# Splitting the next group's first weight item earlier, with six separate hi/lo homes and raw weights released singly

## Chip, cores and metric

The kernel runs on one core of one Trainium2 chip. The metric is device time in microseconds (us) of one execution. The time before is the median of three runs.

## What is computed

Two decoder layers on 512 tokens of width 1024, all in float32. Each layer has a half-step SwiGLU feed-forward part, a mixer (a gated linear recurrence and a sliding-window attention, each with a gate) and a second half-step feed-forward part, all with RMS norms around them:

```
def swiglu(h, w_gate, w_up, w_down):
    return (jax.nn.silu(h @ w_gate) * (h @ w_up)) @ w_down
...
  x += 1/2 * post(SwiGLU_1(pre(x)))
  h  = pre(x);  P = h @ W_in
  x += post( (sigmoid(gA)*A + sigmoid(gB)*B) @ W_out )
  x += 1/2 * post(SwiGLU_2(pre(x)))
```

D_MODEL is 1024 and D_FF is 2816, so that the gate and the up weight have 22 column blocks of 128 each. The weights of one feed-forward part are 66 units of 512 KB, each read from HBM once.

## The kernel before

**Products in three parts.** Every float32 operand is split into a rounded part hi and a rest lo (both float32r), and a product is three matmuls: hi·hi, hi·lo and lo·hi (`mm3`, helper line L116 in the profile). A weight unit is a tile of 128 x 1024 float32. SyncE loads it (L247) into one of four raw buffers (`W32` = 4, tag `w32`). Splitting it takes a copy on ScalarE that writes hi (L354), and for lo one of two ways. Either VectorE subtracts hi from the raw unit (L363), or, for the kinds "v", "a" and "d", ScalarE writes the negative of the raw unit into lo (L358) and GpSimd issues a DMA that adds the raw unit to it (L361, an accumulating DMA from SBUF to SBUF). There are six hi and six lo buffers (`WS` = 6), so at most six split items are in flight.

**The pair phases.** Most of a feed-forward part's gate and up blocks go through `fast` (L1073) and `sevenths` (L1036): two raw units u and u+1 and two halves of the tokens make one 2 x 2 block product that is done with seven half-size products in place of eight. A *group* is one such pair. Its four items are

- a: unit u as it is, lo by the accumulating DMA of 512 KB; products p1 and p2
- b: sums on VectorE (L340, L341), lo by VectorE (L363); products p5 and p7
- c: two more sums (L347, L348), lo by VectorE; products p6 and p4
- d: half of unit u+1, lo by an accumulating DMA of 256 KB; product p3

TensorE takes them in the order a b c d, 84 matmuls of 128 x 256 per group, in an order written out by hand. After c, VectorE combines the results in PSUM (L1063, L1065, L1069, L1070), and ScalarE takes a SiLU (L1084). The next group's items are called a', b', c', d' below. There are four pair phases, one per feed-forward part: the first with 15 groups, the others with 19. In the profile they lie at about 88.7–233.4, 728.0–915.2, 1062.3–1247.0 and 1741.6–1928.0 us. The mixer has four further groups per layer in its gates part (`gates`, L189).

**Order of the work.** `split` (L324) takes the items in the order in which TensorE uses them; `ahead` (L373) calls it whenever fewer than four items (`AHEAD` + 1) lie ahead of the one in use and fewer than six are in flight. In the pair phases (`tight`), ScalarE's and VectorE's instructions of a split are kept in program order, so where `split` is called decides what stands ahead of what on ScalarE, VectorE and GpSimd. Each of these engines and each DMA queue works through its list in order. A raw unit is given back, and the load that takes its buffer issued, at the end of d for both units of the group (L366–371).

Of the kernel before, what the change touches and what calls it, by code (L numbers as in the profile page):

```python
# [8 lines left out]
F32R = mybir.dt.float32r  # L9
# [6 lines left out]
P = 128  # L16
D = 1024
# [19 lines left out]
W32, WS, AHEAD, TAIL, FIRST, EARLY, LATE = 4, 6, 3, 4, 7, 4, 8  # L37
# [9 lines left out]
def trunk(ctx: ExitStack, tc: tile.TileContext, xin, wall, gains, lbT, hgain, sinks, c_dist, c_mask, c_ident, out):  # L47
    nc = tc.nc
    cp = ctx.enter_context(tc.tile_pool(name="cp", bufs=1))
    sb = ctx.enter_context(tc.tile_pool(name="sb", bufs=1))  # L50
# [9 lines left out]
    def nm(s):  # L60
        seq[0] += 1
        return f"{s}_{seq[0]}"
# [18 lines left out]
    class Order:  # L81
        def __init__(self):
            self.t = 0.0
            self.rest = 0.0
            self.cos = []
# [73 lines left out]
    class Stream:  # L159
        def __init__(self):  # L160
            self.n, self.wall = 0, 0
            self.items = []
            self.raw, self.dma = {}, 0
            self.done, self.flight = 0, 0
            self.cur, self.c = 0, 0
            self.src = {}
            self.pinned = False
            self.most = AHEAD
            self.tight, self.gate = False, None
            self.side, self.freed = [], 0  # L170
            self.part = {}

        def plain(self, n, kind="u", at=0):
# [84 lines left out]
        def quarter(self, it):  # L258

            q, u, v, h = it.q, it.u, it.u + it.n, (slice(0, S), slice(S, D))  # L260

            def sums(o, x, y, op):
                for c in range(2):
                    pin(nc.vector.tensor_tensor(o[c], x[c], y[c], op=op))  # L264

            def raw(i):
                self.load(i + 1)
                return [self.raw[i][:, c] for c in h]

            def leave(i):  # L270
                self.raw.pop(i)
                self.freed += 1
                self.load(self.freed + W32)

            if it.kind in ("p1", "p2"):
                w = raw((u if it.kind == "p1" else v) + q)
            elif it.kind in ("p3", "p5"):
                w = self.b22[q]
            elif it.kind == "p7":

                w = self.b12[q]
                if q == 0:
                    sums(w, w, self.b22[q], ALU.add)
            else:
                w = self.b12[q]
            it.hi, it.lo = (sb.tile([P, D + 64], F32R, tag=t, name=nm(t), bufs=WS)[:, it.at : it.at + D] for t in ("whi", "wlo"))
            for c in range(2):
                i = nc.scalar.copy(it.hi[:, h[c]], w[c])  # L288
                if self.pinned:
                    pin(i)  # L290
            if it.kind == "p7" and q + 1 < it.n:
                sums(self.b12[q + 1], self.b12[q + 1], self.b22[q + 1], ALU.add)
            elif it.kind == "p6":
                sums(self.b22[q], self.b22[q], w, ALU.add)
            for c in range(2):
                pin(nc.vector.tensor_tensor(it.lo[:, h[c]], w[c], it.hi[:, h[c]].bitcast(F32), op=ALU.subtract))  # L296
            if it.kind == "p7":

                sums(w, raw(u + q), w, ALU.subtract)
                leave(u + q)  # L300
            elif it.kind == "p5":
                self.b22[q] = None
                if q + 1 < it.n:
                    sums(self.b12[q], raw(v + q), self.b12[q], ALU.add)
                    leave(v + q)
            elif it.kind == "p4":
                self.b12[q] = None
                if q == 0:
                    i = it.n - 1
                    sums(self.b12[i], raw(v + i), self.b12[i], ALU.add)  # L310
                    leave(v + i)
            self.done += 1
            self.flight += 1
# [5 lines left out]
        def product(self):  # L319
            if self.gate:  # L320
                self.gate()
                self.gate = None

        def split(self):  # L324
            it = self.items[self.done]
            if it.kind[0] == "p":
                return self.quarter(it)
            u, last = it.u, it.kind in "uvd"
            self.load(u + (1 if it.kind in "uv" else 2))
            it.hi, it.lo = (sb.tile([P, D + 64], F32R, tag=t, name=nm(t), bufs=WS)[:, it.at : it.at + D] for t in ("whi", "wlo"))  # L330
            w, h = self.raw[u], (slice(0, D // 2), slice(D // 2, D))
            cols = (slice(0, D),)
            if it.kind == "u" and u < 2:
                cols = h
            if it.kind in "bcd":
                v = self.raw[u + 1]
            if it.kind == "b":

                self.t13 = sb.tile([P, D], F32, tag="tt", name=nm("tt"), bufs=2)
                pin(nc.vector.tensor_tensor(self.t13[:, h[0]], w[:, h[0]], v[:, h[0]], op=ALU.add))  # L340
                pin(nc.vector.tensor_tensor(self.t13[:, h[1]], v[:, h[0]], v[:, h[1]], op=ALU.add))  # L341
                w = self.t13
                self.product()
            elif it.kind == "c":

                t = sb.tile([P, D], F32, tag="tt", name=nm("tt"), bufs=2)
                pin(nc.vector.tensor_tensor(t[:, h[0]], self.t13[:, h[0]], v[:, h[1]], op=ALU.add))  # L347
                pin(nc.vector.tensor_tensor(t[:, h[1]], t[:, h[0]], w[:, h[1]], op=ALU.add))  # L348
                w = t
            elif it.kind == "d":  # L350
                w = v
                cols = h[1:]
            for c in cols:
                i = nc.scalar.copy(it.hi[:, c], w[:, c])  # L354
                if u < 6 or self.pinned or self.tight:
                    pin(i)
                if it.kind in "vad":
                    i = nc.scalar.mul(it.lo[:, c], w[:, c], -1.0)  # L358
                    if self.pinned or self.tight:
                        pin(i)  # L360
                    nc.gpsimd.dma_start(it.lo[:, c].bitcast(F32), w[:, c], accum_op=ALU.add)  # L361
                else:
                    self.hold(nc.vector.tensor_tensor(it.lo[:, c], w[:, c], it.hi[:, c].bitcast(F32), op=ALU.subtract))  # L363
            self.done += 1
            self.flight += 1
            if last:  # L366
                nu = u + (1 if it.kind in "uv" else 2)
                for i in range(u, nu):
                    self.raw.pop(i)
                    self.freed += 1  # L370
                self.load(self.freed + W32)

        def ahead(self):  # L373
# [2 lines left out]

        def need(self, i):
            self.ahead()
            while self.done <= i:
                assert self.flight < WS  # L380
                self.split()
            return self.items[i]
# [117 lines left out]
    def pair_split(v, how=split):  # L500
        return how(v, to=(big(F32R, [P, 2, S // 2]), big(F32R, [P, 2, S // 2])))
# [13 lines left out]
    class First(Quarters):  # L515
# [44 lines left out]
        def sums(self):  # L560

            k = len(self.x56)
            a = []
            for i in range(2):
                f = xs[k + 4 * i]
                nc.vector.scalar_tensor_tensor(f, f, g_sb[:, 0, 0, k + 4 * i : k + 4 * i + 1], self.rb, op0=ALU.mult, op1=ALU.mult)
                a.append([f[:, c] for c in HALF])
            self.x124.append([])
            for v in (a[0][0], a[1][0], a[1][1]):
                x = big(F32R, [P, 2, S // 2])  # L570
                split(v, to=(x[:, 0, :], x[:, 1, :]))
                self.x124[k].append(x)
            for x, v in zip((self.x56, self.x37), quarter_sums(a[0][0], a[1][0], a[0][1], a[1][1])):
                x.append(pair_split(v))
# [74 lines left out]
    class Late:  # L649
# [20 lines left out]
        def first(self, k):  # L670
            x = big(F32R, [P, 2, S // 2])
            self.x1.append(split(self.src[k][:, HALF[0]], to=(x[:, 0, :], x[:, 1, :]), hold=pin))
# [979 lines left out]
```

## Time and profile before

| what | value |
|---|---|
| median of three runs | 2052.85 us (2051.64 to 2053.39) |
| profiled execution | 2052.22 us |
| span of its profile | 2050.4 us |
| TensorE busy | 2035.9 us, 99% |
| VectorE, ScalarE, GpSimd busy | 79%, 61%, 13% |
| granted TensorE clock | 0.999 |
| DMA, mean over the span | 160 GB/s |

The span is measured from the first to the last recorded instruction; 1.8 us of the execution lie around it. A timeline row has the start, the duration, the engine, the line and the operation, with output and inputs (buffer numbers left out), and in brackets the idle time ahead of it with what ended that. A window row has the stretch, its length, and for each engine the busy time and, in brackets with an x, the number of instructions. A row of DMA issues has the queue, the count, the size of each and the median time from issue to landing.

### The profile page before, as it was taken

How to read it: one execution, taken by the hardware profiler on the slowest of the kernel's cores; microseconds unless marked ns; L12 is line 12 of the kernel's file. 1: busy time of each engine (PE TensorE's matmuls, PEld its weight loads, DVE VectorE, ACT ScalarE, POOL GpSimd, SP SyncE). 2: the span in 40 equal slices, each digit the busy share in tenths (PEclk: the TensorE clock that was granted, in tenths of full speed). 3: DMA queues.
4: the chain of work that ended last, by engine and by line, in shares of the span. 5: the costliest groups of instructions: out<-in, count | busy, mean ns of one | idle time of the engine just before them, and what ended most of it. 6: DMA issues, size and time to landing. Idle time of an engine off the chain costs nothing. (4 is left out here: it accounts for less than half of the span.)

```text
span 2050.4 us, 36557 instructions
## 1 busy us (share of the span) xinstructions
PE 2035.9 (99%) x13553; PEld 1820.7 (89%) x13553; DVE 1623.6 (79%) x2894; ACT 1250.1 (61%) x2213; POOL 267.6 (13%) x318
## 2 busy tenths in 40 slices
PE   9999999999999999999999999999999999999998
PEld 8899978877888999998899998888778989999977
DVE  5887889767676778888988878987686858788888
ACT  7566687446355556658866566864554545665684
POOL 0111140000000011113201111400000100111140
PEclk9999999999999999999999999999999999999999
DMA  8577798322237367778757878872122563777794
GB/s 257 146 189 193 184 195 238 117 64 71 73 94 215 114 147 190 189 190 205 203 154 188 193 187 205 181 229 92 62 73 62 136 194 102 181 188 190 184 201 123
DMA packets 166802, 328.07 MB, mean 160 GB/s; under 512 B 19072, under 2 KB 85088, under 8 KB 166624
## 3 DMA queue, kind: packets, MB, share of 16 engines
q1 hardware_dynamic: 122416, 228.16, 33.2%
q0 software_dynamic: 44064, 97.54, 28.2%
q8 instruction: 106, 1.74, 0.3%
q14 instruction: 72, 0.59, 0.1%
q10 hardware_dynamic: 144, 0.05, 0.0%
HBM read 213.43 MB, written 14.73 MB: 111 GB/s over the span
## 5 line engine op out<-in xcount | busy, mean ns | idle before, releaser
L116 PE MATMUL acc<-s,whi 128*128 128x256 f32 (+1 forms) x4998 | 1027.5, 305 | 0.0
L116 PEld LDWEIGHTS acc<-s,whi 128*128 128x128 f32 x4998 | 794.7, 188 | 46.5 <-issue 3.2
L116 PE MATMUL acc<-s,wlo 128*128 128x256 f32 (+1 forms) x2488 | 757.0, 304 | 3.3 <-DMA wlo<-w 2.9
L116 PEld LDWEIGHTS acc<-s,wlo 128*128 128x128 f32 x2488 | 469.1, 189 | 28.7 <-DMA wlo<-w 5.0
L116 PE MATMUL acc<-whi,s 128*128 128x512 f32 x1360 | 442.4, 393 | 2.6 <-DVE s L433 1.8
L354 ACT CAST whi<-w 128x1024 fp32r<-128x1024 f32 (+1 forms) x310 | 286.5, 928 | 148.2 <-PE acc L116 105.2
L354 ACT CAST whi<-tt 128x1024 fp32r<-128x1024 f32 x160 | 168.0, 1050 | 250.2 <-DVE tt L348 164.7
L361 POOL DMA_DIRECT2D wlo<-w x178 | 154.0, 867 | 1235.6 <-DVE wlo L363 504.8
L116 PEld LDWEIGHTS acc<-whi,s 128*128 128x128 f32 x1360 | 255.0, 188 | 61.4 <-issue 3.2
L363 DVE TENSOR_TENSOR wlo<-tt,whi 128x1024 fp32r<-128x1024 f32 x160 | 196.0, 1225 | 131.9 <-ACT whi L354 126.0
L116 PE MATMUL acc<-wlo,s 128*128 128x512 f32 x680 | 266.4, 392 | 0.9 <-DVE wlo L296 0.9
L116 PE MATMUL aux<-s,whi 128*128 128x256 f32 (+1 forms) x1296 | 230.0, 280 | 0.0
L363 DVE TENSOR_TENSOR wlo<-w,whi 128x1024 fp32r<-128x1024 f32 (+1 forms) x132 | 157.3, 1205 | 73.9 <-ACT whi L354 73.6
L116 PEld LDWEIGHTS aux<-s,whi 128*128 128x128 f32 x1296 | 197.0, 188 | 1.1 <-issue 0.5
L116 PE MATMUL aux<-s,wlo 128*128 128x256 f32 (+1 forms) x648 | 181.1, 279 | 0.0
L116 PEld LDWEIGHTS acc<-wlo,s 128*128 128x128 f32 x680 | 127.8, 188 | 29.8 <-DVE wlo L296 5.1
L358 ACT ACTIVATE wlo<-w 128x1024 fp32r<-128x1024 f32 (+1 forms) x178 | 153.7, 863 | 0.0
L116 PE MATMUL aux<-whi,s 128*128 128x512 f32 x432 | 144.1, 391 | 0.0
L444 POOL DMA_DIRECT2D s<-s x128 | 111.1, 971 | 216.1 <-ACT s L432 98.1
L116 PEld LDWEIGHTS aux<-s,wlo 128*128 128x128 f32 x648 | 122.1, 188 | 0.5 <-DMA wlo<-w 0.2
L296 DVE TENSOR_TENSOR wlo<-s,whi 128x512 fp32r<-128x512 f32 x160 | 102.7, 685 | 9.9 <-ACT whi L288 6.3
L432 ACT CAST s<-s 128x512 fp32r<-128x512 f32 (+1 forms) x140 | 70.8, 547 | 44.8 <-DVE s L491 39.3
(184 smaller groups left out, 2468.7 us busy)
## 6 DMA issues: line engine op xcount, KB each, us to landing
w<-wall SPq DMA_DIRECT2D x267, 512.0 KB, 4.2
wlo<-w POOLq DMA_DIRECT2D x98, 512.0 KB, 5.2
w<-wall SPq DMA_DIRECT2D x224, 128.0 KB, 3.5
wlo<-w POOLq DMA_DIRECT2D x80, 256.0 KB, 3.3
s<-wall SPq DMA_DIRECT2D x128, 128.0 KB, 4.4
s<-s POOLq DMA_DIRECT2D x64, 256.0 KB, 4.9
x_d<-s SPq DMA_DIRECT2D x48, 256.0 KB, 4.1
s<-x_d SPq DMA_DIRECT2D x48, 256.0 KB, 5.1
```

The costliest lines, as they stand in the source:

```text
L116: nc.tensor.matmul(o, lhsT, rhs, start=start, stop=stop)
L296: pin(nc.vector.tensor_tensor(it.lo[:, h[c]], w[c], it.hi[:, h[c]].bitcast(F32), op=ALU.subtract))
L354: i = nc.scalar.copy(it.hi[:, c], w[:, c])
L358: i = nc.scalar.mul(it.lo[:, c], w[:, c], -1.0)
L361: nc.gpsimd.dma_start(it.lo[:, c].bitcast(F32), w[:, c], accum_op=ALU.add)
L363: self.hold(nc.vector.tensor_tensor(it.lo[:, c], w[:, c], it.hi[:, c].bitcast(F32), op=ALU.subtract))
L432: (hold or ws.hold)(nc.scalar.copy(hi, src))
L444: nc.gpsimd.dma_start(lo.bitcast(F32), src, accum_op=ALU.add)
```

## The change

It has three parts.

1. **Order of splits.** A plan replaces the running index: where an item a follows an item d, it is split ahead of the two items that come before it. The order a b c d a' b' c' d' becomes a b a' c d b' a'' c' d' and so on. TensorE's order is the same.
2. **Homes.** The six hi and lo buffers get tags of their own (`whi0` … `wlo5`). An item takes, of those whose last item is used up, the one whose item came first in TensorE's order; before, the pool gave the six out under one tag. `quarter` does the same.
3. **Raw units one by one.** Unit u is given back, and a load issued into its buffer, after c; unit u+1 after d.

```
+        def home(self, it):
+
+            k = min((k for k in range(WS) if not self.own[k] or self.own[k].left <= 0), key=lambda k: self.own[k].i if self.own[k] else -1)
+            self.own[k] = it
+            it.hi, it.lo = (sb.tile([P, D + 64], F32R, tag=f"{t}{k}", name=nm(t))[:, it.at : it.at + D] for t in ("whi", "wlo"))
+
         def split(self):
-            it = self.items[self.done]
+            if not self.plan:
+                for i, it in enumerate(self.items):
+                    it.i = i
+                    self.plan.append(i)
+                    if it.kind == "a" and self.items[i - 1].kind == "d":
+                        self.plan[i - 2 : i + 1] = [i, i - 2, i - 1]
+            it = self.items[self.plan[self.done]]
...
-            it.hi, it.lo = (sb.tile([P, D + 64], F32R, tag=t, name=nm(t), bufs=WS)[:, it.at : it.at + D] for t in ("whi", "wlo"))
-            w, h = self.raw[u], (slice(0, D // 2), slice(D // 2, D))
+            self.home(it)
+            w, h = self.raw.get(u), (slice(0, D // 2), slice(D // 2, D))
...
-            if last:
-                nu = u + (1 if it.kind in "uv" else 2)
-                for i in range(u, nu):
-                    self.raw.pop(i)
-                    self.freed += 1
+            if it.kind in "uvcd":
+                self.raw.pop(u + (it.kind == "d"))
+                self.freed += 1
                 self.load(self.freed + W32)
...
-            while self.done <= i:
+            while not hasattr(self.items[i], "hi"):
```

On ScalarE, one group of the first pair phase before: the copy of b', a copy out of PSUM (L1051), the copies of c' and d', the multiplication of d', then the pair of a'' (`whi_2036`, `wlo_2037`, from raw unit `w_336`), then the SiLU.

```order
L354 CAST whi_1936<-tt_1938 128x1024
L1051 COPY s_1931<-acc_1927 128x256
L354 CAST whi_1969<-tt_1971 128x1024
L354 CAST whi_2000<-w_317_1753 128x512
L358 ACTIVATE wlo_2001<-w_317_1753 128x512
L354 CAST whi_2036<-w_336_1878 128x1024
L358 ACTIVATE wlo_2037<-w_336_1878 128x1024
L1084 ACTIVATE m_2018<-m_2018 128x512
```

The same place of the changed kernel, where the split's copy is L367, its multiplication L371, the PSUM copy L1062 and the SiLU L1095:

```order
L367 CAST whi_1936<-tt_1938 128x1024
L1062 COPY s_1931<-acc_1927 128x256
L367 CAST whi_1969<-w_336_1878 128x1024
L371 ACTIVATE wlo_1970<-w_336_1878 128x1024
L367 CAST whi_1998<-tt_2000 128x1024
L367 CAST whi_2034<-w_320_1785 128x512
L371 ACTIVATE wlo_2035<-w_320_1785 128x512
L1095 ACTIVATE m_2016<-m_2016 128x512
```

The pair of instructions that reads `w_336`, the whole unit of a'', has moved from behind d' to ahead of c'. Nothing is added and nothing taken away.

On GpSimd, the accumulating DMAs of three groups in the same phase before; those of 128x512 belong to items d, those of 128x1024 to items a:

```order
L361 DMA wlo_1366<-w_217_1118 128x512
L361 DMA wlo_1402<-w_236_1243 128x1024
L361 DMA wlo_1493<-w_237_1245 128x512
L361 DMA wlo_1529<-w_256_1370 128x1024
L361 DMA wlo_1620<-w_257_1372 128x512
L361 DMA wlo_1656<-w_276_1497 128x1024
```

And of the changed kernel, where the line is L374:

```order
L374 DMA wlo_1335<-w_236_1243 128x1024
L374 DMA wlo_1400<-w_220_1150 128x512
L374 DMA wlo_1462<-w_256_1370 128x1024
L374 DMA wlo_1527<-w_240_1277 128x512
L374 DMA wlo_1589<-w_276_1497 128x1024
L374 DMA wlo_1654<-w_260_1404 128x512
```

Within each group the whole unit's DMA (`w_236`) now stands ahead of the half unit's (`w_220`, the same half unit as `w_217` of before under another number). VectorE's order in the pair phases and SyncE's order of loads are the same as before; in the mixer's gates part the rows of the two items move likewise on ScalarE, VectorE and GpSimd.

More of the change, by code (lines that the diff above doesn't have):

```diff
@@ L170, in __init__ @@
             self.side, self.freed = [], 0
+            self.own, self.plan = [None] * WS, []
             self.part = {}
@@ L322, in product @@
                 self.gate = None
+        def home(self, it):
+            k = min((k for k in range(WS) if not self.own[k] or self.own[k].left <= 0), key=lambda k: self.own[k].i if self.own[k] else -1)
+            self.own[k] = it
+            it.hi, it.lo = (sb.tile([P, D + 64], F32R, tag=f"{t}{k}", name=nm(t))[:, it.at : it.at + D] for t in ("whi", "wlo"))
         def split(self):
-            it = self.items[self.done]
+            if not self.plan:
[5 more added lines that the diff above has]
+            it = self.items[self.plan[self.done]]
             if it.kind[0] == "p":
                 return self.quarter(it)
-            u, last = it.u, it.kind in "uvd"
+            u = it.u
             self.load(u + (1 if it.kind in "uv" else 2))
-            it.hi, it.lo = (sb.tile([P, D + 64], F32R, tag=t, name=nm(t), bufs=WS)[:, it.at : it.at + D] for t in ("whi", "wlo"))
-            w, h = self.raw[u], (slice(0, D // 2), slice(D // 2, D))
+            self.home(it)
+            w, h = self.raw.get(u), (slice(0, D // 2), slice(D // 2, D))
             cols = (slice(0, D),)
```

## The prediction

> **What bounds the kernel now.** I read the page first, then the waits of TensorE, then windows over the four pair phases, and last one group in the timelines. The page's busy times and its two large DMA queues (packets, MB, share of 16 engines' span):
>
> ```profile
> PE 2035.9 (99%) x13553; PEld 1820.7 (89%) x13553; DVE 1623.6 (79%) x2894; ACT 1250.1 (61%) x2213; POOL 267.6 (13%) x318
> q1 hardware_dynamic: 122416, 228.16, 33.2%
> q0 software_dynamic: 44064, 97.54, 28.2%
> ```
>
> TensorE is busy nearly always, so there is little idle time to win. The queues give prices: q0, the accumulating DMAs, took 28.2% of 2050.4 us for 97.54 MB, 5.93 us per MB, so 3.1 us of all 16 engines for a 512 KB item and 1.55 us for 256 KB; q1, the loads, 680.7 us for 228.16 MB, 1.56 us per unit. What TensorE and its weight loads wait for of DMA (us, times, longest):
>
> ```profile
> PE acc L116 <- DMA wlo<-w: 2.9, 4, 1.6
> PEld acc L116 <- DMA wlo<-w: 5.0, 9, 1.8
> ```
>
> Not above 8 us, and the two lists overlap. But waiting is not all that a stage can lose. The four pair phases, then one stretch of 37 us, then five other stretches inside the phases:
>
> ```profile
> 88.70:233.40 144.70, 144.70 (x1262) 144.70 (x1261) 115.98 (x163) 88.99 (x122) 24.95 (x29) 1.00 0.79 191
> 728.00:915.20 187.20, 187.04 (x1599) 186.49 (x1599) 150.53 (x210) 115.22 (x158) 31.85 (x37) 1.00 0.78 188
> 1062.30:1247.00 184.70, 182.66 (x1599) 181.52 (x1598) 147.71 (x208) 113.16 (x156) 31.84 (x37) 1.00 0.77 187
> 1741.60:1928.00 186.40, 185.83 (x1599) 185.33 (x1598) 149.72 (x210) 115.03 (x158) 31.84 (x37) 1.00 0.78 189
> 147.00:184.00 37.00, 37.00 (x329) 37.00 (x328) 30.78 (x44) 22.22 (x30) 6.88 (x8) 1.00 0.79 186
> 184.00:234.00 50.00, 50.00 (x424) 49.91 (x423) 39.88 (x57) 32.02 (x45) 7.74 (x9) 1.00 0.78 194
> 747.00:758.00 11.00, 10.84 (x91) 10.44 (x89) 8.61 (x13) 6.36 (x9) 1.72 (x2) 1.00 0.77 211
> 786.00:915.00 129.00, 129.00 (x1096) 128.88 (x1095) 104.14 (x145) 79.81 (x109) 21.53 (x25) 1.00 0.78 190
> 1761.00:1801.00 40.00, 39.95 (x338) 39.74 (x337) 31.73 (x45) 24.61 (x33) 6.88 (x8) 1.00 0.79 192
> 1858.00:1928.00 70.00, 69.49 (x590) 69.29 (x589) 56.19 (x79) 44.16 (x61) 11.18 (x13) 1.00 0.78 193
> ```
>
> The same matmuls run at two rates under a granted clock of 1.00 throughout: 37.00/329 = 112.5 ns each at first, 129.00/1096 = 117.7 ns in the longest of the others. The slow rate sets in at one of the waits for an accumulating DMA and stays until the next; what decides it, the profile does not say. The five slow stretches are 300 us, and at about 3.8% cost some 11 us.
>
> How long should a phase be? One group as TensorE runs it: the first use of d's lo, the first of the next a's lo, and the same a in the group before.
>
> ```profile
> 117.50 0.28 PE L116 MATMUL acc<-s,wlo 128*128 128x256 f32 x1
> 125.66 0.28 PE L116 MATMUL aux<-s,wlo 128*128 128x256 f32 x1
> 127.02 0.28 PE L116 MATMUL acc<-s,wlo 128*128 128x256 f32 x1
> ```
>
> From a to a it is 127.02 − 117.50 = 9.52 us (84 matmuls; at the slow rate 84 x 117.7 ns = 9.89). By 9.52 us, 15 groups need 142.8 us and 19 need 180.9; the windows are 1.9, 6.3, 3.8 and 5.5 us longer, **17.5 us in all**. No change in these phases can win more. VectorE's own round shows where it begins:
>
> ```profile
> 98.75 0.68 DVE L1063 TENSOR_TENSOR m<-acc,s 128x512 f32<-128x512 f32 x1
> 108.51 0.68 DVE L1063 TENSOR_TENSOR m<-acc,s 128x512 f32<-128x512 f32 x1
> 118.22 0.68 DVE L1063 TENSOR_TENSOR m<-acc,s 128x512 f32<-128x512 f32 x1
> ```
>
> It takes 9.71 to 9.76 us per group, 0.19 more than a fast TensorE. Each group therefore eats 0.19 us of every margin, until the tightest is gone and TensorE waits.
>
> **The change part by part.** Which margin is tightest? ScalarE in one group (c, d, then the next a), GpSimd's two DMA issues (d, then a), and their issue-to-landing times (d, a, and the load issued at c):
>
> ```profile
> 113.22 0.36 ACT L1051 COPY s<-acc 128x256 f32<-128x256 f32 x1
> 115.99 1.05 ACT L354 CAST whi<-tt 128x1024 fp32r<-128x1024 f32 x1 [2.41 <-PE aux L116]
> 118.00 1.03 ACT L354 CAST whi<-w 128x1024 fp32r<-128x1024 f32 x1
> 118.94 1.06 ACT L358 ACTIVATE wlo<-w 128x1024 fp32r<-128x1024 f32 x1
> 118.39 0.86 POOL L361 DMA_DIRECT2D wlo<-w  x1 [6.96 <-DVE wlo L363]
> 120.29 0.86 POOL L361 DMA_DIRECT2D wlo<-w  x1 [1.03 <-DVE m L1069]
> wlo<-w POOLq DMA_DIRECT2D x1, 256.0 KB, 3.2
> wlo<-w POOLq DMA_DIRECT2D x1, 512.0 KB, 5.1
> w<-wall SPq DMA_DIRECT2D x1, 512.0 KB, 3.5
> ```
>
> Item a lands at 120.29 + 5.1 = 125.4 for a use at 127.02: margin 1.6. Item d lands at 118.39 + 3.2 = 121.6 for 125.66: margin 4.1. So a's DMA is the tight one, and d's has 2.5 us more.
>
> *Moving a ahead of c.* ScalarE idles 2.41 us before c's copy. The pair now starts where L1051 ends, at about 113.5; two instructions that start 0.94 apart end at about 115.5, 0.4 us before c's copy can start at 115.99. So c is not delayed, VectorE's round stays at 9.71, and a's DMA is issued 0.3 us after its multiplication, as at 120.29, at about 115.8: **4.5 us earlier**. It doesn't land 4.5 earlier, since it now shares the engines with the load issued at c. The trace has one such meeting, in the third phase, where a DMA of an a at 1116.11 fell upon a load, both landed late, and TensorE waited:
>
> ```profile
> wlo<-w POOLq DMA_DIRECT2D x1, 512.0 KB, 6.2
> w<-wall SPq DMA_DIRECT2D x1, 512.0 KB, 5.7
> 1122.32 0.38 PE L116 MATMUL acc<-s,wlo 128*128 128x256 f32 x1 [1.58 <-DMA wlo<-w]
> ```
>
> At 6.2 us a lands at 122.0, 3.4 us before it did: its margin becomes about 5.0.
>
> *What is late next: d.* Its issue stays at 118.39, but its DMA is now behind a's in GpSimd's queue. From below its landing does not move (3.2 us); from above it waits for a's whole landing at 122.0 and then takes its own 3.2, so 125.2, 3.6 later. I take 122.0 plus its 1.55 us of data plus a little for the completion, 123.8, **2.2 later**: margin 4.1 − 2.2 = 1.9. So the tightest margin is 1.9 in place of 1.6; from both sides between 0.5 and 4.1. This is nearly an exchange of one late wait for another.
>
> The Trainium skill, page "DMA: Bandwidth & Descriptors", section "Queues, rings and completion order", has each DMA engine consume a ring's descriptors in order and take turns between rings; by that rule d waits for a's data while load and a share, which speaks against this change, and the meeting at 1116 agrees with it (6.2 and 5.7 us against 5.1 and 3.5).
>
> *Raw units.* SyncE's order is unchanged, and a load can't start before the last reader of its buffer is done, which is c's sum at 115.9 either way: cost nothing. The load issued at c takes 5.7 and lands at 121.7, for a copy now at 113.5 + 9.7 = 123.2; 1.5 us are left.
>
> *Homes.* TensorE's order and the number of buffers are the same, and at 113.5 TensorE is in c, so that a's and b's homes of that group are free. I take nothing. From above, if the moved copy waited for c to be used up (d's first use is 117.50 − 1.36 = 116.1), it would be 2.6 late, 2.2 beyond ScalarE's slack, in each of 72 groups: 158 us, to which I give no chance of its own, since two homes are free.
>
> *Gates part.* There one a landed 8.8 us after its issue, and TensorE waited:
>
> ```profile
> 593.54 0.86 POOL L361 DMA_DIRECT2D wlo<-w  x1 [2.00 <-PE acc L116]
> 602.42 0.39 PE L116 MATMUL acc<-s,wlo 128*128 128x256 f32 x1 [0.46 <-DMA wlo<-w]
> ```
>
> That item is split earlier too: −0.5, from both sides −0.5 to +0.5.
>
> *Phase starts.* ScalarE's pair of about 2 us moves there too, while TensorE still works on older items; I take 0, from −2 to +2 over the four.
>
> **Sum.** Gates −0.5. The meeting of the third phase was a's wait of 1.58 and goes: −1.6. The margin is 0.3 larger, once per phase: −1.2. So the first wait comes 0.3/0.19 = 1.6 groups later in each phase, and where the slow rate follows, as in three of the four, that saves 0.37 x 1.6 = 0.6: −1.8. Together −5.1, from 2052.2 (the profiled execution, its span of 2050.4 and 1.8 around it) to 2047.1. The median of the runs, 2052.85, lies 0.6 above that execution: **2047.7 us**. Own range −1 to −9.
>
> **The rivals.**
>
> 1. *Fast rate to the end.* If d's margin stays at 2 and more, or the remaining waits happen to leave the fast rate, the 11 us of slow stretches go as well: with 0.19 us per group after the margin is used up (some 7 us left of 17.5), −10, at best −16. For it: the whole third phase kept its fast rate through several waits. Against it: 5 stretches elsewhere did not. By the Trainium skill's page "DMA: Bandwidth & Descriptors", section "Anatomy of one DMA", a software DMA takes about 2.0 us plus bytes/436e3, so an estimate of 3.2 us for 512 KB; d would then hardly be held up, and this case would follow, but the rows of 5.1 and 6.2 disagree.
> 2. *d takes a's place, and worse* (the slower side). d's delay is 3.6 us, not 2.2. Margins of 0.5 are gone within three groups, TensorE waits early in each phase, and the slow rate stays to its end: 0.37 x 16 = 6 us in each long phase, 4 in the first, 22 together; with 1 us of first waits in each 26 in place of 17.5, so **+8**, 2061. It decides from a delay of d of about 3 us on. For it: a, d and two loads are 3.1 + 1.55 + 2 x 1.56 = 7.8 us of data per 9.7 us, and in the new order they follow one another nearly without a gap.
> 3. *The load comes late for the moved copy.* If it lands over 1.9 us later than at 5.7 (1.5 left, and 0.4 on ScalarE), c's copy waits in order behind a's, and each 0.3 us beyond costs 72 groups x 0.3 = 20 us. Against it: no load here was that late in the pair phases.
> 4. *Nothing happens*: one wait is exchanged for another of the same size, and the rates fall alike: within 1 us.
>
> **How the numbers follow.** Forecast 0.42, fast rate 0.17, d worse 0.22, late load 0.05, nothing 0.14. A measurement of this kernel can tell about 0.2%, 4.1 us, from no change. Two thirds of the forecast (−1 to −9) lie beyond it: faster 0.28 + 0.17 = 0.45; same 0.13 of it, the 0.14, and a little of d worse, 0.30; slower 0.25. The range takes in the forecast, the −10 of the fast rate and most of rival 2: 2039 to 2060.
>
> **What would show it.** Right: in the pair phases a's DMA is issued about 2.6 us before d's, lands some 6 us later and no longer ends a wait; what waits of TensorE remain name d, a matmul into aux; d lands some 5.4 us after its issue; VectorE's round is still 9.71. Wrong: waits for a remain, c's copy on ScalarE starts late, or windows of 129 us show other counts than between 1096 and 1147. The sum rests most on d's delay and on the rate that follows a wait; if either is off, so is it.

## The result, and the profile after

The changed kernel takes 2081.35 us (median of four runs, 2074.22 to 2083.63), against 2053.12 us before: a ratio of 1.0132, 95% interval 1.0119 to 1.0145, so 28 us slower. The forecast was 2047.7 with a range up to 2060. The profiled execution took 2083.63 us, 31.4 more than that of before.

First the page of the changed kernel, with the busy times and the DMA issues (queue, count, size, median us from issue to landing):

```profile
PE 2045.5 (98%) x13553; PEld 1821.7 (88%) x13553; DVE 1625.3 (78%) x2894; ACT 1252.2 (60%) x2213; POOL 268.2 (13%) x318
w<-wall SPq DMA_DIRECT2D x267, 512.0 KB, 4.5
wlo<-w POOLq DMA_DIRECT2D x98, 512.0 KB, 7.4
wlo<-w POOLq DMA_DIRECT2D x80, 256.0 KB, 6.8
```

No engine has more instructions than before; TensorE's busy time, whose ends the profile models, grew by 9.6 us, the others' by about 2 or less. Item d's DMA takes 6.8 us to land; on the page of before it was 3.3, and a's went from 5.2 to 7.4. The lists of waits, TensorE's first and then ScalarE's (us, times, longest):

```profile
PE aux L116 <- DMA wlo<-w: 21.0, 29, 1.8
```

```profile
ACT whi L367 <- DMA w<-wall: 46.3, 32, 5.7
```

The same line of the kernel before, for ScalarE:

```profile
ACT whi L354 <- DMA w<-wall: 17.2, 11, 4.4
```

TensorE's waits for an item a (a matmul into acc) are gone. In their place stand 29 waits for d (into aux), and ScalarE waits 29 us more for raw weights. VectorE has such a wait as well, at the first sum of an item b (L353, L340 of before), 14.5 us in all; before the change that sum had none inside the pair phases:

```profile
DVE tt L353 <- DMA w<-wall: 14.5, 11, 3.3
```

The four pair phases of the changed kernel, between the same matmuls as in the windows of before:

```profile
91.90:241.00 149.10, 147.01 (x1262) 145.95 (x1261) 115.64 (x162) 86.00 (x118) 23.28 (x27) 1.00 0.75 178
737.20:930.00 192.80, 187.69 (x1598) 185.91 (x1597) 150.37 (x211) 112.99 (x155) 30.20 (x35) 1.00 0.74 178
1078.00:1272.20 194.20, 186.58 (x1598) 184.19 (x1597) 150.12 (x211) 112.57 (x154) 30.21 (x35) 1.00 0.73 174
1765.80:1958.70 192.90, 186.23 (x1598) 183.36 (x1597) 150.18 (x211) 112.71 (x154) 30.18 (x35) 1.00 0.73 175
```

They are 4.4, 5.6, 9.5 and 6.5 us longer than before, 26 of the 31. The first window begins 3.2 us later, so that 3 us are lost at the very start. The slow matmul rate is not it: 2979 of the 128x256 matmuls were followed by the next after 117 to 119 ns, 3165 before. What grew is the time by which these matmuls followed one another later than 118 ns, from 8.5 to 35.0 us in the whole profile.

One group of the first phase shows one way in which the time is lost. VectorE's round from L1074 (L1063 of before) to L1074, then ScalarE at the same place, then three DMA issues ahead of it in the order of time: an a at 129.03, the load of the next a's raw unit at 129.53, and a d at 131.65.

```profile
131.48 0.68 DVE L1074 TENSOR_TENSOR m<-acc,s 128x512 f32<-128x512 f32 x1
...
138.18 0.69 DVE L361 TENSOR_TENSOR tt<-tt,w 128x512 f32<-128x512 f32 x1
140.82 1.23 DVE L376 TENSOR_TENSOR wlo<-tt,whi 128x1024 fp32r<-128x1024 f32 x1 [1.95 <-ACT whi L367]
141.96 0.68 DVE L1074 TENSOR_TENSOR m<-acc,s 128x512 f32<-128x512 f32 x1
```

```profile
136.19 0.36 ACT L1062 COPY s<-acc 128x256 f32<-128x256 f32 x1
137.84 1.05 ACT L367 CAST whi<-w 128x1024 fp32r<-128x1024 f32 x1 [1.29 <-DMA w<-wall]
138.80 1.05 ACT L371 ACTIVATE wlo<-w 128x1024 fp32r<-128x1024 f32 x1
139.75 1.03 ACT L367 CAST whi<-tt 128x1024 fp32r<-128x1024 f32 x1
```

```profile
wlo<-w POOLq DMA_DIRECT2D x1, 512.0 KB, 8.6
w<-wall SPq DMA_DIRECT2D x1, 512.0 KB, 8.2
wlo<-w POOLq DMA_DIRECT2D x1, 256.0 KB, 7.2
```

The load took 8.2 us, where the load issued at c took 3.5 before. It landed at 137.8, and ScalarE's copy of a, which now stands ahead of c's, started only then. So c's copy started at 139.75, 0.9 us after its sum was done (138.18 + 0.69), VectorE waited 1.95 us in place of 1.17, and its round was 141.96 − 131.48 = 10.48 us in place of 9.71. The same stretch of VectorE before:

```profile
117.08 1.23 DVE L363 TENSOR_TENSOR wlo<-tt,whi 128x1024 fp32r<-128x1024 f32 x1 [1.17 <-ACT whi L354]
```

Over the four phases the mean round rose from 9.77 to 10.18 us: 68 x 0.41 = 28 us. Leaving out the last round of each phase, 19 rounds are longer than 9.9 us. In 15 of them the copy of a starts within 0.2 us of its load's landing; before the change, no copy of an a in these phases waited for its load.

The second way costs about as much, and it does not go through the moved copy. In ten of the 19 rounds VectorE's first sum of b waited for a raw unit, 13.4 us in all, about half of the 28. Among them are the four whose copy of a was not late, and these are 12.0 to 13.1 us long. The unit is the other one, u+1, whose buffer comes free when d lands. VectorE in the longest of them, then its d (issued at 768.96) and its load (issued at 776.62):

```profile
784.29 0.69 DVE L353 TENSOR_TENSOR tt<-w,w 128x512 f32<-128x512 f32 x1 [3.31 <-DMA w<-wall]
wlo<-w POOLq DMA_DIRECT2D x1, 256.0 KB, 7.3
w<-wall SPq DMA_DIRECT2D x1, 512.0 KB, 7.6
```

Item d landed at 776.3, its load at 784.2, and VectorE stood 3.31 us. In the group of before, d and the load behind it took 3.2 and 5.2 us. SyncE issues its loads in one list, so a late d also holds up the load of c: here that one was issued at 777.07, 0.9 us after c's sum was done.

### The profile page after: what moved, and what is told of

The parts are those of the page before. It is cut to its first block, busy times and chain, and to the rows that moved or that the text cites. A ratio compares the mean times of both kernels' runs of the same rounds, so it can differ in the third digit from the quotient of the medians.

```text
span 2081.8 us, 36351 instructions
## 1 busy us (share of the span) xinstructions
PE 2045.5 (98%) x13553; PEld 1821.7 (88%) x13553; DVE 1625.3 (78%) x2894; ACT 1252.2 (60%) x2213; POOL 268.2 (13%) x318
## 5 line engine op out<-in xcount | busy, mean ns | idle before, releaser
L367 ACT CAST whi<-w 128x1024 fp32r<-128x1024 f32 (+1 forms) x310 | 287.8, 932 | 220.0 <-PE acc L116 124.9
L374 POOL DMA_DIRECT2D wlo<-w x178 | 154.3, 868 | 1266.1 <-ACT wlo L371 1017.0
L367 ACT CAST whi<-tt 128x1024 fp32r<-128x1024 f32 x160 | 167.7, 1048 | 110.7 <-DVE tt L354 56.2
L116 PE MATMUL aux<-s,wlo 128*128 128x256 f32 (+1 forms) x648 | 185.8, 287 | 21.5 <-DMA wlo<-w 21.0
L1095 ACT ACTIVATE m<-m 128x512 f32<-128x512 f32 x72 | 45.6, 633 | 195.9 <-DVE m L1081 195.9
L371 ACT ACTIVATE wlo<-w 128x1024 fp32r<-128x1024 f32 (+1 forms) x178 | 153.9, 864 | 0.0
```

Of the source, the lines that this page charges most:

```text
L116: nc.tensor.matmul(o, lhsT, rhs, start=start, stop=stop)
L1095: ws.hold(nc.scalar.activation(out=m[:, 0:2, :], in_=m[:, 0:2, :], func=AF.Silu))
```

## The experiments

A first theory, **A**, was that the new order costs the time through the DMAs: d stands behind a in one queue, and the load that waits for d's landing joins the pile. The rivals were **B**, that the six named homes make copies wait, and **C**, that giving raw units back singly bunches the loads. Later **D** was added: VectorE's round, not the late DMA that TensorE names, had set the length of a pair phase already before the change. All medians stand beside a median of before of 2052.5 to 2052.7 us from the same chips. In the text below, the phases' and the start's shares are from the profiled execution against that of before, between the same matmuls of TensorE.

**Order undone, the rest kept.**

```
-                    if it.kind == "a" and self.items[i - 1].kind == "d":
-                        self.plan[i - 2 : i + 1] = [i, i - 2, i - 1]
```

> Homes and single release kept, items split in the old order a b c d. Theory A (the new order costs the time: d's accumulating DMA stands behind a's, and the load that waits for d joins the pile) expects the pair phases as before the change, and only the 3 us lost near 12 to 60 us, where one early copy moved ahead of two others: 2054 to 2057 us, no wait of TensorE for d. Theory B (six named homes make copies wait for TensorE in every group) and theory C (single release bunches the loads) expect most of the loss to stay: 2070 to 2082 us.

2058.32 us, ratio 1.0027 (1.0016 to 1.0037). The waits for d are gone, 3.1 us are lost at the start and 7.1 in the phases, of which 4.7 come back behind them; VectorE's mean round is 9.77 us, as before the change. The time is 1 us above what A expected and far below B and C: the order costs over 20 of the 28.

**Both raw units given back after d, order and homes kept.**

```
-            if it.kind in "uvcd":
-                self.raw.pop(u + (it.kind == "d"))
-                self.freed += 1
+            if it.kind in "uvd":
+                nu = u + (1 if it.kind in "uv" else 2)
+                for i in range(u, nu):
+                    self.raw.pop(i)
+                    self.freed += 1
                 self.load(self.freed + W32)
```

> New order and homes kept, both raw units given back after d as before. Theory A expects 2075 to 2084 us, as the changed kernel, since the loads still wait for the same readers. Theory C expects the pair phases to lose 10 us or more less: below 2070 us.

2078.6 us, ratio 1.0127 (1.011 to 1.0144). C falls: the single release is worth no more than 3 us.

**One shared tag in place of the homes, order and single release kept.**

```
-            self.home(it)
+            it.hi, it.lo = (sb.tile([P, D + 64], F32R, tag=t, name=nm(t), bufs=WS)[:, it.at : it.at + D] for t in ("whi", "wlo"))
```

> New order and single release kept, the six hi and lo buffers given out by the pool under one tag again. Theory B expects a clear gain over the changed kernel, 2050 to 2060 us. Theory A expects no gain in the pair phases, 2070 to 2085 us, with the 3 us at the start gone; and if the pool's rotation ties d's buffer to the a that TensorE uses after it, more waits than in the changed kernel, 2090 us or above.

2077.17 us, ratio 1.0113 (1.0098 to 1.0128). The start's 3 us are won back (−0.3 against before), and the phases lose 23 us. B falls, and so does the guess that the pool's rotation would make it worse.

**d's DMA issued ahead of a's, everything else as changed.**

```
+                    g = lambda o=it.lo[:, c], v=w[:, c]: pin(nc.gpsimd.dma_start(o.bitcast(F32), v, accum_op=ALU.add))
+                    if it.kind == "a" and it.i and self.items[it.i - 1].kind == "d":
+                        self.late = g
+                    else:
+                        g()
+                        if it.kind == "d" and self.late:
+                            self.late()
+                            self.late = None
```

> As the changed kernel, ScalarE still splits a ahead of c, but GpSimd issues d's DMA ahead of a's (all accumulating DMAs kept in program order). Theory A expects d to land some 3 to 4 us after its issue again, the load that waits for it to start 3 us earlier, a to land about 2 us earlier than before the change, and no wait for either: 2040 to 2055 us with the 3 us at the start still in it. Theories B and C expect 2070 us or more, since homes and release are as changed.

2056.71 us, ratio 1.0019 (1.001 to 1.0028), 1.7 us above A's range and far below the rivals'. On its page d lands after 3.3 us again, and of the accumulating DMAs TensorE's list names only those of a:

```profile
wlo<-w POOLq DMA_DIRECT2D x98, 512.0 KB, 5.7
wlo<-w POOLq DMA_DIRECT2D x80, 256.0 KB, 3.3
```

```profile
PE acc L116 <- DMA wlo<-w: 2.7, 5, 0.8
```

ScalarE's early copy of a is still there, so the early copy alone is harmless; the place of a's DMA does the harm. VectorE's waits for raw weights at the sum of b fall from 14.5 to 1.1 us. A holds for the loss. But a's DMA is issued 1.4 us earlier than before the change, and the phases gain only 1.3 us in all. That was the first sign that a's DMA had not been their bound.

**The same, with the early copies at the start kept in order.** In the changed kernel ScalarE took the copy of the seventh unit ahead of the fifth's and sixth's, and waited for it; then the copies of four units came at once:

```profile
25.59 1.05 ACT L367 CAST whi<-w 128x1024 fp32r<-128x1024 f32 x1 [5.68 <-DMA w<-wall]
26.54 2.19 ACT L473 ACTIVATE s<-s 128x512 f32<-128x512 f32 x4
28.64 3.93 ACT L367 CAST whi<-w 128x1024 fp32r<-128x1024 f32 x4
```

TensorE paid for it on its next two uses:

```profile
29.72 0.74 PE L116 MATMUL acc<-s,whi 128*128 128x512 f32 x2 [1.04 <-ACT whi L367]
31.28 0.51 PE L116 MATMUL acc<-s,wlo 128*128 128x512 f32 x1 [0.82 <-DVE wlo L376]
```

```
-                if u < 6 or self.pinned or self.tight:
+                if u < 8 or self.pinned or self.tight:
```

> As the run with d's DMA first, and ScalarE's copies of the seventh and eighth unit at the very start kept in program order (the condition u < 6 made u < 8). If the 3 us at 12 to 60 us come from the copy that moved ahead of two others, they go: 2052 to 2054 us, equal to the kernel before within 0.1%. If they come from the homes themselves, nothing changes: 2056 to 2057 us.

2053.43 us, ratio 1.0002 (0.9992 to 1.0011): the 3.3 us are the order of these copies, which the homes changed and nothing kept.

**Five raw buffers on the changed kernel, and on the kernel before as a control.**

```
-W32, WS, AHEAD, TAIL, FIRST, EARLY, LATE = 4, 6, 3, 4, 7, 4, 8
-SLOTS = 61
+W32, WS, AHEAD, TAIL, FIRST, EARLY, LATE = 5, 6, 3, 4, 7, 4, 8
+SLOTS = 59
```

> The changed kernel with five raw buffers in place of four, and 59 working tiles in place of 61 to make room. A load then no longer waits for the d of the group just split. Theory A1 (d is late because it stands behind a's whole DMA in one queue) expects d still to land 5 us or more after its issue and TensorE still to wait for it, 2066 to 2080 us. Theory A2 (d is late because its landing releases a load that falls on the next a and d, and the other load comes too late for ScalarE's copy) expects most of the waits to go, 2052 to 2062 us.

2058.63 us, ratio 1.0025 (1.0016 to 1.0034). TensorE's wait for d and ScalarE's for raw weights:

```profile
PE aux L116 <- DMA wlo<-w: 9.2, 14, 1.6
```

```profile
ACT whi L367 <- DMA w<-wall: 10.0, 6, 5.9
```

Item d lands no earlier (6.8 us by its page), and yet 22.7 of the 28 us are gone, with most of ScalarE's wait for raw weights and all of VectorE's at the sum of b; the mean round is 9.79 again. So what costs most is not that TensorE waits for d, but that the loads come too late, for the moved copy on ScalarE and for the sum of b on VectorE.

> Control for the run with five raw buffers: the kernel before with five raw buffers and 59 working tiles. If five buffers by themselves neither win nor lose, 2050 to 2056 us, and what that run won over the changed kernel (22 us) is the load that came too late. If this run is below 2048 us, part of it was something else.

2048.0 us, ratio 0.9978 (0.9968 to 0.9988), below the range expected: five buffers win 4.5 us by themselves. Taken off, the late loads stand for about 18 of the 28 us, the start for 3, and d's place for about 7; this split assumes that the shares add.

**a's DMA in two halves**, the first as early as in the changed kernel, the second behind d's (copies pinned).

```
+                    if it.kind == "a" and it.i and self.items[it.i - 1].kind == "d":
+                        g(h[0])
+                        self.late = lambda: g(h[1])
```

> As the run with d's DMA first and the copies pinned, but a's accumulating DMA of 512 KB is cut into two of 256 KB: the first half issued as early as in the changed kernel, ahead of d's, the second half right behind d's. Theory A1 expects d to stand behind 256 KB only: to land about 4 us after its issue (3.3 alone, 6.8 behind 512 KB), and TensorE to wait little: 2045 to 2053 us. Theory A2, by which any early part of a falls on the loads, expects d at 5 us or more and 2055 us or above.

2053.4 us, ratio 1.0003 (0.9993 to 1.0012), at the edge of A1's range. TensorE takes 8.5 us less for the phases than before, the least so far, and the down projections behind them take all of it back. There it waits for the split of the down weights:

```profile
PE acc L116 <- ACT whi L289: 5.8, 4, 1.6
```

The rounds on VectorE were as long as ever (9.79 us), so VectorE and ScalarE arrived at that work no sooner. This gave theory D.

**The kernel before, with a's DMA in two halves one behind the other.**

```
+                    for e in h if it.kind == "a" else (c,):
+                        nc.gpsimd.dma_start(it.lo[:, e].bitcast(F32), w[:, e], accum_op=ALU.add)
```

> The kernel before, with a's accumulating DMA cut into two of 256 KB, issued one behind the other; nothing else moved. TensorE uses the second half 1.4 us after the first, so if a wait for half the columns ends with their half, a's margin grows by about 1.4 us and most of the first waits in the pair phases go: 2040 to 2050 us. If both halves land together, or a matmul waits for both, it is the kernel before: 2052 to 2054 us.

2055.06 us, ratio 1.0009 (1.0 to 1.0019). A miss: no gain, and its profile has more waits for a (8.2 us in place of 2.9). A wider margin for a is worth nothing in this way either.

**A shorter round, nothing else.** In the pair phases the copies and subtractions of b and c are cut into halves, so that VectorE starts on one half while ScalarE copies the other.

```
+            if it.kind in "bc" and self.tight:
+                cols = h
```

> The kernel before, with ScalarE's copies and VectorE's subtractions of items b and c in the pair phases cut into halves of 512 columns, so that each engine starts on a half while the other works on the next. Theory D (VectorE's round of 9.71 us per group, longer than TensorE's 9.52, sets the length of a pair phase, whatever TensorE's waits name) expects the round to fall below 9.5 us and up to 68 x 0.25 = 17 us to be won: 2036 to 2046 us. If the waits for a's DMA are a bound of their own, the time stays at 2050 to 2054 us with more waits for it; if the extra instructions cost more than the overlap, 2055 us or more.

2025.53 us, ratio 0.987 (0.9855 to 0.9884): 27 us faster than the kernel before, more than expected. The four phases, then TensorE's list of waits, then VectorE between L348 and the next round:

```profile
88.10:230.30 142.20, 142.20 (x1257) 142.20 (x1256) 122.28 (x192) 94.97 (x150) 24.94 (x29) 1.00 0.82 194
722.30:903.40 181.10, 181.10 (x1600) 181.06 (x1599) 156.67 (x248) 122.28 (x194) 31.82 (x37) 1.00 0.83 198
1049.60:1230.50 180.90, 180.90 (x1599) 180.90 (x1598) 156.47 (x247) 121.65 (x193) 31.84 (x37) 1.00 0.82 195
1721.20:1902.30 181.10, 181.10 (x1599) 181.10 (x1598) 156.64 (x247) 122.06 (x194) 31.81 (x37) 1.00 0.82 197
```

```profile
PE aux L116 <- DVE eps_t L139: 1.1, 1, 1.1
PE acc L126 <- DVE s L865: 1.0, 2, 0.5
PE acc L116 <- DVE wlo L296: 0.2, 1, 0.2
```

```profile
103.28 0.69 DVE L348 TENSOR_TENSOR tt<-tt,w 128x512 f32<-128x512 f32 x1
104.00 1.34 DVE L365 TENSOR_TENSOR wlo<-tt,whi 128x512 fp32r<-128x512 f32 x2
105.26 0.69 DVE L1065 TENSOR_TENSOR m<-acc,s 128x512 f32<-128x512 f32 x1
```

The subtraction follows the sum without the 1.17 us that VectorE idled there before. VectorE's mean round falls from 9.77 to 9.43 us, 68 x 0.34 = 23 us over the phases. Each long phase is 19 x 9.53 us, TensorE never idles in it, and every wait for an accumulating DMA is gone, though nothing was done about those DMAs. The phases give 17.2 us of the 17.5 that the prediction had counted, and another 10 come from the work behind them, which VectorE and ScalarE now reach sooner.

D holds for the round: before, it was 9.71 us in the third phase, where next to no matmul ran at the slow rate, and also in the second, where 73% of them did. But the 17.2 us on TensorE are not the round alone. Next to no matmul of the four phases runs at the slow rate now; before, some 2500 did, at 4.5 ns more each (113.1 and 117.6 ns, as worked out at the end), which is 11 us. Whether the short round brings the fast rate is not shown, and the last control below speaks against it.

**The same cut with d's DMA first, and on the changed kernel.**

> The same cut on top of the run with d's DMA first and the copies pinned, where a's DMA is issued 1.4 us earlier than before. Theory D expects at least what the cut wins on the kernel before, and 0 to 6 us more, since a's margin now counts: 2032 to 2044 us. If a's DMA is no bound even with the shorter round, the two runs are equal within 3 us.

2024.8 us, ratio 0.9866 (0.9851 to 0.9881): equal to the cut alone. Even with the short round, a's earlier issue is worth nothing.

> The same cut on the changed kernel. Its rounds are stretched by loads that land too late for ScalarE's copy; with a shorter round the loads have less time, not more. If the late load is the bound, the cut wins less than 10 us here: 2070 to 2082 us. If the length of the round was what made the loads collide, 2050 to 2065 us.

2060.9 us, ratio 1.0045 (1.003 to 1.006). The cut wins 20 us, and the time lies in the second range; yet the loads still collide, as the first had it: ScalarE's wait for raw weights grows from 46.3 to 65.9 us and VectorE's at the sum of b from 14.5 to 56.9. Neither expectation was right as a whole. The mean round is 9.90, and 35 us to the cut alone remain (4.4 of them at the start).

**What remains, taken apart.** On the changed kernel, cut and with the early copies pinned: five raw buffers in the first run; in the second four buffers, and d's lo by VectorE's subtraction, so that d has no DMA. The third is the control, the cut kernel of before with five buffers.

```
-                if it.kind in "vad":
+                if it.kind in "va":
```

> The changed kernel, pinned and cut, with four raw buffers, but d's lo made by VectorE's subtraction (128x512, 0.7 us more on VectorE per group, round still near TensorE's 9.52), so that there is no DMA of d: none stands behind a's, and the load that waited for d's landing starts about 5 us earlier. If those two are the whole loss, 2020 to 2032 us. If a's DMA beside a load is enough to make the load late, the long rounds stay and the time is 2040 us or more.

2026.41 us, ratio 0.9871 (0.9856 to 0.9886), though VectorE has 0.7 us more per group. Without d's DMA the whole loss is gone, with a's copy and a's DMA as early as in the changed kernel. The edit also takes d's multiplication (0.63 us per group) off ScalarE; what that is worth by itself was not tried.

> The changed kernel with the early copies pinned, the copies and subtractions of b and c cut into halves, and five raw buffers (59 working tiles). With the rounds short and the early copies in order, only d's place behind a is left of the change, for the load has a buffer in hand. If the late load was the whole of the rest, 2018 to 2027 us, like the cut alone or better; if d's place in the queue costs by itself, TensorE still waits for d and the time is 2030 to 2045 us.

> Control for the first of these three and the fastest guess: the kernel before, cut, with five raw buffers. With the round at TensorE's 9.52 there is little left to wait for: equal to the cut alone within 4 us, 2020 to 2027 us.

The first took 2037.3 us (2028.95 to 2040.8), the control 2029.82 (2022.67, 2022.77, 2036.88 and 2038.67). Both scatter more than the effect in question, so the ranges expected decide nothing. The control's profiled execution, one of its longer ones, shows why: two of its phases lie at the slow matmul rate, without a wait (172.0 us for 1463 matmuls), another at the fast one (163.0 us for 1441):

```profile
728.00:900.00 172.00, 172.00 (x1463) 172.00 (x1462) 144.24 (x230) 112.06 (x177) 30.18 (x35) 1.00 0.81 192
1740.00:1912.00 172.00, 172.00 (x1463) 172.00 (x1462) 143.74 (x230) 112.19 (x178) 29.50 (x35) 1.00 0.80 192
1067.00:1230.00 163.00, 163.00 (x1441) 163.00 (x1440) 142.14 (x227) 109.64 (x174) 30.21 (x35) 1.00 0.84 200
```

In the profiled execution of the first run (2028.95 us) the phases are 16.2 us shorter than before, 1 less than with the cut alone, with one wait of 0.4 us for d. In that execution d's place by itself costs 1 us or so; in how far the others differ by rate alone stays open.

## Why the prediction was wrong, point by point

- **What bounds the kernel.** The rows were read rightly: a round of 9.71 us on VectorE against 9.52 on TensorE. The conclusion was not drawn. If each round is 0.19 us longer than TensorE needs, the round is the bound and a's DMA only the place where TensorE notices it; a wider margin delays the first wait and is handed back behind the phase, as the halves of a showed (8.5 us gained, all returned). "So the first wait comes 0.3/0.19 = 1.6 groups later", −1.2 and −1.8, had no value. That 17.5 us was the most to be won in the phases fits; the cut won 17.2 of it there, some of it by the matmul rate.
- **Moving a ahead of c.** The order on ScalarE and the issue of a came as predicted, 2.6 us ahead of d's in the group shown. "So c is not delayed, VectorE's round stays at 9.71" failed: 10.18 on average.
- **Raw units: this is the step that failed.** "The load issued at c takes 5.7 and lands at 121.7, for a copy now at 113.5 + 9.7 = 123.2; 1.5 us are left." In the 19 long rounds it took 8.4 us (median). The price of 5.7 was from a meeting of one load with one a. In the new order a second load is there too: the one that waits for d's landing, and d now lands 3.5 us later, when the next a and the next load are issued. The prediction put the raw units at "cost nothing" by the load at c alone. It had d 2.2 us later itself, but gave no price to the load behind d, whose reader is VectorE's sum of b. The chain is d late, its load late, and then two ways to a long round: the other load is late too, and with it the moved copy and c; or VectorE's sum of b waits (13.4 us in ten rounds). In how far it feeds itself was not measured. Taking away d's DMA, or issuing it ahead of a's, or adding a buffer broke it. The first way was rival 3, with its mechanism and its point of decision (1.9 us later than 5.7; it was 2.7), priced at 20 us for 0.3 us beyond per group and given a chance of 0.05 with the reason that "no load here was that late in the pair phases". That was evidence from the old order, on a step that changes the order. The second way was in no rival.
- **d.** It lands 6.8 us after its issue in place of 3.3 (medians of the page): 3.5 later, at the upper bound of 3.6, not the 2.2 taken. Rival 2 was thus right on d, yet its price came by the slow rate, which hardly changed. The time went through the round. The Trainium skill's page "DMA: Bandwidth & Descriptors", section "Queues, rings and completion order", by which each DMA engine takes a ring's descriptors in order, agrees with the runs: 3.3 us with d's DMA first, 6.8 behind a's. The formula on the same page of the Trainium skill, section "Anatomy of one DMA", an estimate of 3.2 us for 512 KB, does not: 5.2 before, 7.4 after.
- **Homes.** "I take nothing" held for the rounds: 9.77 us with the homes and the old order, as before. The 3.2 us at the start were not priced at all: the homes changed the order of three early copies on ScalarE, and the prediction looked at the order in the pair phases and the gates part alone.
- **Gates part.** The wait of 0.46 us in layer 0 is gone as predicted, but 0.4 us were lost just ahead of it, so that 0.2 remain, and 0.2 were lost in layer 1.

## What to carry to other kernels

When two engines work in rounds, compare their periods before reading the waits: here the longer round was the bound, and the list of waits of the engine with the shorter one named only where it caught up. Before an early operation is moved ahead on an engine that works in order, look at what it reads, not only at who reads it. If a transfer will land later, follow what waits for its landing, down to the load that takes its buffer and that load's reader. Ask which transfers the new order starts together; a landing time from the old order did not bound them here. The cheapest gain in a chain of two engines handing a tile to and fro was to hand it over in halves: 27 us here, with 264 more instructions.

## What was not expected of the hardware

TensorE's two rates for the same 128x256 matmul, 113.1 and 117.6 ns at a granted clock of 1.00 (163.0/1441 and 172.0/1463), are not bound to waits: in the last control whole phases took the one or the other without any wait, and its four runs fall in two pairs, 2022.7 and 2037 to 2039. What chooses the rate was not found. By the Trainium skill's page "TensorE: Matmul & The Clock Gate", section "Wait — 56ns, not 53.3ns?", a warm matmul starts every N ÷ 2.4 GHz + 2.5 ns, an estimate of 109 ns for 256 columns; neither rate agrees. By the totals of the two queues on the page of before, an estimate, an accumulating DMA of 512 KB from SBUF to SBUF keeps all 16 engines about 3.1 us, twice as long as a load of the same size from HBM (1.56); one of them beside two loads is then 6.2 us of a round of 9.7.
